# Two-head scores in the halves of the array, softmax sums dividing y, and six w buffers in a decoder layer

## The chip, the cores and the metric

The kernel runs on one core of a Trainium2 chip. The metric is the device time of one execution in microseconds (us); the median of the runs is compared. Engines are named as in the profile: PE is the matrix engine (TensorE), PEld its weight loads, DVE VectorE, ACT ScalarE, POOL GpSimd, SP the engine that issues nearly all DMAs.

## The reference

One decoder layer on x[1024 x 1024], float32. A combined input projection feeds three branches, whose outputs are concatenated and projected back; a gated MLP (ConvFFN) and a last norm follow. Cut to what matters here:

```
h = rmsnorm(x);  p = h @ w_in
# 6 "fox" heads of 64: causal, with a decay bias c_q - c_k
s = q @ k.T * 64**-0.5 + c_q - c_k;  s = where(k <= q, s, -inf)
ya = rmsnorm(softmax(s) @ v)
# 6 dilated heads of 64: three windows (128,1), (512,4), (2048,16) mixed by their sums:
# a softmax over all keys with a fixed table added to the scores
yb = rmsnorm(dilated_mixture(q, k, v))
# 256 channels, 31 taps
yc = silu(layernorm(causal_dwconv(gv * sigmoid(gg), conv_w) + conv_b))
x = x + concat(ya, yb, yc) @ w_o
```

## The kernel before, in words

Every matmul whose operands are float32 is made of three products of high and low parts (hi·hi, lo·hi, hi·lo); a helper issues them as L116, L117 and L118. Activations lie transposed, features on the partitions. The attention stage, about 125 to 527 us of the span, goes over six pairs of heads (pair 0 to 2 fox, 3 to 5 dilated). For each pair a generator `attention` goes over four blocks of 256 queries (i) and both heads (h): `scores` makes two tiles w[128 queries x up to 1024 keys], in chunks of at most 512 keys: two matmuls into a PSUM slot (L379, L380; fox adds a mask, L382), a DVE operation that adds the bias and takes the minimum (L385, since q is negated), the exponential with its row sum on ACT (L390), then the reciprocal of the sum on DVE (L392) and the division of w on POOL (L393). `turn` transposes w (L405) and splits it into hi and lo (L409 on ACT, L410 on DVE), `values` multiplies with V (L421, L422), and L444, L445 add the two halves into y. PSUM has five slots for scores and transposes together, SBUF four buffers (tag "sp") for w.

L379 contracts over 128 rows: QA holds the 64 rows of a head's q_hi and under them its q_lo, KA twice k_hi. L380 contracts over 64 rows, q_hi with k_lo (in KL).

A mixer, `mix`, draws units of other matmul work (the projections of the next pair, norms, the first output projections) between the steps of `attention`, by weights given to each step. The order on each engine is fixed when the program is built: a scheduler goes through the instructions by their dependences, by priority and by when it expects buffers to come free, and each engine then runs its list in order.

The convolution (`conv_taps`) is written behind pair 0: one DVE operation per channel block starts the sum (L506) and 30 more each add a tap (L508), into yc0 and yc1, which have buffers of their own. Its norm (`conv_norm`) is mixed into pair 1. yc is needed again behind pair 4, where it is split for the output projection.

```
yc = [bp.tile([P, S], F32, tag=f"yc{c}", name=f"yc{c}") for c in range(2)]
...
V.tensor_scalar(y, u, col(wc + 30), col(C_CB + c), op0=ALU.mult, op1=ALU.add)
for d in range(1, 31):
    V.scalar_tensor_tensor(y[:, d:], u[:, 0:S - d], col(wc + 30 - d), y[:, d:],
                           op0=ALU.mult, op1=ALU.add)
```

Of the kernel before, what the change touches and what calls it, by code (L numbers as in the profile page):

```python
# [60 lines left out]
def hybrid_trunk(ctx: ExitStack, tc: tile.TileContext, xT, par, win, wvf, wo, wup, wdn,  # L61
# [88 lines left out]
    with ExitStack() as cb_:  # L150
# [70 lines left out]
        V.tensor_copy(idb, idf)  # L221

        V.tensor_scalar(mkb, trf, -BIG, BIG, op0=ALU.mult, op1=ALU.add)
# [16 lines left out]
        yc = [bp.tile([P, S], F32, tag=f"yc{c}", name=f"yc{c}") for c in range(2)]  # L240
# [43 lines left out]
        def proj_q(pr, out):  # L284
            QA, QB = pair_tile(f"QA{pr}"), pair_tile(f"QB{pr}")
            out["Q"] = (QA, QB)
            w = load_chunk(win[pr if pr < 3 else pr + 3], 8, f"wq{pr}")
            for i in range(2):
                ps = mm_ps(f"qps{pr}_{i}")
                yield from mm_gen(ps, w, xs, HS[i])  # L290
                qs = bp.tile([P, HALF], F32, tag="ev", name=f"qs{pr}_{i}", bufs=2)
                V.scalar_tensor_tensor(qs, ps, -0.125, r1b[:, HS[i]], op0=ALU.mult, op1=ALU.mult)
                h = HS[i]
                A.copy(QA[0:64, h], qs[0:64])
                A.copy(QB[64:128, h], qs[64:128])
                G.tensor_sub(QA[64:128, h], qs[0:64], QA[0:64, h].bitcast(F32))
                G.tensor_sub(QB[0:64, h], qs[64:128], QB[64:128, h].bitcast(F32))

        def proj_k(pr, out):
            KA = pair_tile(f"KA{pr}")  # L300
            if pr in (2, 4):
                kk = bp.tile([P, 2, S], F32R, tag="VS", name=f"KBL{pr}", bufs=3)
                KB, KL = kk[:, 0, :], kk[:, 1, :]
            else:
                KB, KL = pair_tile(f"KB{pr}"), pair_tile(f"KL{pr}")
            out["K"], out["KL"] = (KA, KB), KL
            w = load_chunk(win[pr + 3 if pr < 3 else pr + 6], 8, f"wk{pr}")
            for i in range(2):
# [8 lines left out]
                A.copy(KA[0:64, h], ks[0:64])  # L317
                A.copy(KB[64:128, h], ks[64:128])
                G.tensor_scalar(KA[64:128, h], ks[0:64], 1.0, 0.0, op0=ALU.mult, op1=ALU.add)
                G.tensor_scalar(KB[0:64, h], ks[64:128], 1.0, 0.0, op0=ALU.mult, op1=ALU.add)  # L320
                V.tensor_sub(KL[0:64, h], ks[0:64], KA[0:64, h].bitcast(F32))
                V.tensor_sub(KL[64:128, h], ks[64:128], KB[64:128, h].bitcast(F32))
# [35 lines left out]
        def attention(pr, a, bias, fox, y, ahead):  # L358
            Q, K, KL, VSp = a["Q"], a["K"], a["KL"], a["V"]
            steps = [(i, h) for i in range(NT // 2) for h in range(2)]  # L360
            ws = {}

            def scores(n):
                i, h = steps[n]
                ro = slice(64 * h, 64 * h + 64)
                nm = f"{pr}_{i}_{h}"
                ws[n] = []
                for j in range(2):
                    qi = 2 * i + j
                    nk = P * (qi + 1)  # L370
                    qsl = slice(P * qi, nk)
                    w = sp_tile(f"w{nm}_{j}")
                    mn = None
                    for c0 in range(0, nk, HALF):
                        m = min(HALF, nk - c0)
                        ks = slice(c0, c0 + m)
                        ps = s_ps(f"s{nm}_{j}_{c0}")
                        diag = fox and c0 + m == nk
                        T.matmul(ps[:, 0:m], lhsT=Q[h][:, qsl], rhs=K[h][:, ks], start=True, stop=False)  # L379
                        T.matmul(ps[:, 0:m], lhsT=Q[h][ro, qsl], rhs=KL[ro, ks], start=False, stop=not diag)  # L380
                        if diag:
                            T.matmul(ps[:, m - P:m], lhsT=mkb, rhs=idb, start=False, stop=True)  # L382
                        m2 = bp.tile([P, 1], F32, tag="mn", name=f"mn{nm}_{j}_{c0}", bufs=8)
                        b = bias[h][:, ks] if fox else bias[h][:, S - nk + c0:S - nk + c0 + m]
                        V.tensor_tensor_reduce(out=w[:, ks], in0=ps[:, 0:m], in1=b, scale=1.0,  # L385
                                               scalar=3.0e38 if mn is None else mn,
                                               op0=ALU.add, op1=ALU.min, accum_out=m2)
                        mn = m2
                    den = bp.tile([P, 1], F32, tag="den", name=f"den{nm}_{j}", bufs=4)
                    A.activation(w[:, 0:nk], w[:, 0:nk], AF.Exp, scale=-1.0, bias=mn, accum_out=den)  # L390
# [35 lines left out]
            for n, (i, h) in enumerate(steps):  # L426
# [893 lines left out]
```

## Time and profile before

| | |
|---|---|
| median of 3 runs (lowest to highest) | 1322.84 us (1322.1 to 1322.9) |
| the profiled execution: its own time / its span | 1320.88 us / 1319.1 us |
| PE busy, whole span | 1240.6 us (94%) |
| DVE / ACT / POOL busy | 1062.8 / 635.9 / 602.6 us |
| granted TensorE clock, mean | 0.973 |

The span is the profiled part of that execution. Busy times are sums over instructions; matmuls overlap each other in the pipeline, so the price of a matmul is better read from the distance between the starts of neighbours.

### The profile page before, as it was taken

What the parts mean: (1) busy time and instruction counts of PE and PEld (TensorE: products, weight loads), DVE (VectorE), ACT (ScalarE), POOL (GpSimd) and SP (SyncE); (2) the same over time, 40 slices, a digit from 0 to 9 for tenths busy, and PEclk for the clock granted to TensorE, in tenths of its full rate; (3) what the DMA queues carried; (4) which work ended last, traced back from release to release, by engine and by line L of the source; (5) the groups of instructions that cost most, each with busy time, mean ns of one, the idle gap of its engine ahead of it and who ended that gap; (6) DMA issues with size and microseconds to landing.
All of it is one profiled execution on the core that took longest, in us unless ns stands there. A gap on an engine that the chain in (4) does not pass through costs nothing.

```text
span 1319.1 us, 17062 instructions
## 1 busy us (share of the span) xinstructions
PE 1240.6 (94%) x5809; PEld 987.8 (75%) x5809; DVE 1062.8 (81%) x1589; ACT 635.9 (48%) x1146; POOL 602.6 (46%) x517
## 2 busy tenths in 40 slices
PE   7899899999999999998697999999999979999996
PEld 5887677777777767775476888888888858787795
DVE  8799797756665576789989888888888898978876
ACT  6413456566555564425344455544554554534333
POOL 4566455643655342357751111111111375767754
PEclk9999899999999999998798999999999989999998
DMA  7002010101000112220022323313332454535213
GB/s 236 21 17 81 9 56 18 48 17 49 17 18 28 42 33 100 76 95 16 0 81 104 112 104 112 112 70 111 104 116 104 129 190 147 188 92 160 64 31 128
DMA packets 56407, 106.69 MB, mean 81 GB/s; under 512 B 5456, under 2 KB 25600, under 8 KB 56320
## 3 DMA queue, kind: packets, MB, share of 16 engines
q1 hardware_dynamic: 55744, 105.32, 23.7%
q8 instruction: 46, 0.75, 0.2%
q14 instruction: 41, 0.34, 0.1%
q10 hardware_dynamic: 576, 0.28, 0.1%
HBM read 82.75 MB, written 22.83 MB: 80 GB/s over the span
## 4 chain that ended last, share of the span: by engine, by line
PE 65%; DVE 20%; POOL 5%; issue 5%; DMA 3%; ACT 2%; SPq 0%; DVEq 0%; ACTq 0%; POOLq 0%
PE mA L116 5%; PE mA L117 5%; PE mA L118 5%; PE m L118 4%; PE m L117 4%; PE m L116 4%; PE s L380 4%; PE pt L405 3%; PE d L118 3%; PE d L117 3%; PE d L116 3%; PE s L379 3%; DVE yc L508 3%; PE av L422 2%; PE av L421 2%
## 5 line engine op out<-in xcount | busy, mean ns | idle before, releaser
L828 POOL TENSOR_TENSOR wl<-a,wh 128x512 fp32r<-128x512 f32 x48 | 69.7, 1453 | 294.6 <-ACT wh L827 282.4
L393 POOL TENSOR_SCALAR w<-w,rd 128x128 f32<-128x128 f32 (+3 forms) x96 | 77.0, 806 | 137.7 <-DVE rd L392 80.9
L118 PE MATMUL d<-hc,wld 128*128 128x512 f32 x252 | 101.8, 404 | 7.9 <-POOL wld L828 7.9
L410 DVE TENSOR_TENSOR pl<-pt,ph 128x512 fp32r<-128x512 f32 (+1 forms) x120 | 74.9, 634 | 38.6 <-ACT ph L409 35.5
L117 PE MATMUL d<-hc,whd 128*128 128x512 f32 x252 | 100.4, 398 | 5.3 <-DVE hc L1146 5.3
L390 ACT ACTIVATE w<-w,mn 128x128 f32<-128x128 f32 (+3 forms) x96 | 74.4, 775 | 61.6 <-DVE mn L385 58.5
L116 PE MATMUL d<-hc,whd 128*128 128x512 f32 x252 | 100.2, 398 | 0.8 <-ACT whd L827 0.8
L117 PE MATMUL m<-t,wh 128*128 128x512 f32 x208 | 83.0, 399 | 7.5 <-DVE t L741 7.5
L508 DVE SCALAR_TENSOR_TENSOR yc<-gv,prm,yc 128x1023 f32<-128x1023 f32 (+29 forms) x60 | 89.0, 1483 | 0.9
L116 PE MATMUL m<-t,wh 128*128 128x512 f32 x208 | 82.2, 395 | 4.2 <-ACT t L740 4.2
L409 ACT CAST ph<-pt 128x512 fp32r<-128x512 f32 (+1 forms) x120 | 63.8, 541 | 44.6 <-PE pt L405 31.8
L118 PE MATMUL m<-t,wl 128*128 128x512 f32 x208 | 82.5, 397 | 1.4 <-POOL wl L828 1.4
L405 PE MATMUL pt<-idf,w 128*128 128x128 f32 x432 | 70.8, 279 | 8.1 <-POOL w L393 7.7
L827 ACT CAST wh<-a 128x512 fp32r<-128x512 f32 x84 | 52.2, 621 | 41.5 <-issue 24.3
L828 POOL TENSOR_TENSOR wld<-a_d,whd 128x384 fp32r<-128x384 f32 x48 | 57.3, 1196 | 21.4 <-ACT whd L827 21.3
L118 PEld LDWEIGHTS d<-hc,wld 128*128 128x128 f32 x252 | 48.5, 193 | 23.7 <-POOL wld L828 13.9
L422 PE MATMUL av<-pl,VS 128*128 128x256 f32 x240 | 61.1, 289 | 3.2 <-DVE pl L410 3.2
L421 PE MATMUL av<-ph,VS 128*128 128x256 f32 x240 | 63.8, 285 | 0.2
L116 PE MATMUL mA<-t,wh 128*128 128x512 f32 x144 | 56.9, 395 | 6.4 <-ACT u L1034 6.4
L405 PEld LDWEIGHTS pt<-idf,w 128*128 128x128 f32 x432 | 50.4, 142 | 15.7 <-POOL w L393 11.1
L828 DVE TENSOR_TENSOR wl<-s,wh 128x512 fp32r<-128x512 f32 x54 | 42.9, 795 | 22.7 <-ACT wh L827 22.7
L117 PEld LDWEIGHTS d<-hc,whd 128*128 128x128 f32 x252 | 48.5, 192 | 16.8 <-DVE hc L1146 6.4
(465 smaller groups left out, 4035.7 us busy)
## 6 DMA issues: line engine op xcount, KB each, us to landing
a<-in_wup SPq DMA_DIRECT2D x88, 256.0 KB, 2.7
tr<-td SPq DMA_DIRECT2D x27, 512.0 KB, 3.8
a_d<-in_wdn SPq DMA_DIRECT2D x48, 192.0 KB, 2.4
td<-cv SPq DMA_DIRECT2D x9, 512.0 KB, 2.6
td<-ta SPq DMA_DIRECT2D x9, 512.0 KB, 3.5
td<-tb SPq DMA_DIRECT2D x9, 512.0 KB, 3.6
x<-in_xT SPq DMA_DIRECT2D x8, 512.0 KB, 3.7
outT<-fo SPq DMA_DIRECT2D x8, 512.0 KB, 3.0
```

What stands on the lines that cost most here:

```text
L116: T.matmul(ps, lhsT=wh, rhs=xh[:, sl], start=first, stop=False, **kw)
L117: T.matmul(ps, lhsT=wh, rhs=xl[:, sl], start=False, stop=False, **kw)
L118: T.matmul(ps, lhsT=wl, rhs=xh[:, sl], start=False, stop=last, **kw)
L390: A.activation(w[:, 0:nk], w[:, 0:nk], AF.Exp, scale=-1.0, bias=mn, accum_out=den)
L393: G.tensor_scalar(w[:, 0:nk], w[:, 0:nk], rd, 1.0, op0=ALU.mult, op1=ALU.mult)
L405: T.transpose(pt[:, P * b:P * b + P], ws[n][j][:, P * kt:P * kt + P], idf)
L409: A.copy(ph[:, 0:w], pt[:, 0:w])
L410: V.tensor_sub(pl[:, 0:w], pt[:, 0:w], ph[:, 0:w].bitcast(F32))
L421: T.matmul(o, lhsT=vt, rhs=phl[0][:, r], start=kt == 0, stop=False)
L422: T.matmul(o, lhsT=vt, rhs=phl[1][:, r], start=False, stop=kt == 2 * i + 1)
L508: V.scalar_tensor_tensor(y[:, d:], u[:, 0:S - d], col(wc + 30 - d), y[:, d:], op0=ALU.mult, op1=ALU.add)
L828: eng.tensor_sub(lo, t, hi.bitcast(F32))
```

## The change

Four things are changed.

1. Q and K of a pair are kept as QH, QL, KH, KL, both heads one above the other (64 rows each). `scores(qi)` now makes one block of 128 queries for both heads: three products for each head, all over 64 rows, head 0 in the upper and head 1 in the lower rows, in turn. Each chunk takes two PSUM slots. The mask is two 64-row matmuls for each head.
2. w is no longer divided. The row sums are kept in `den`; `sums` takes the reciprocals of four blocks and two heads at once, transposes them and stores them to DRAM; `divide` loads them back, spread over the partitions, and multiplies 256 columns of y by them on DVE. L392 and L393 are gone.
3. The tag "sp" has six buffers instead of four, and yc0 and yc1 are taken from it too. yc is stored to DRAM after pair 1 and loaded into two "sp" tiles behind pair 4. From pair 2 on, the next scores are written before the transposes of the step instead of behind them.
4. KL is computed on POOL with the full 128 rows, and the weights of the mixer are new.

```diff
-            return bp.tile(shape or [P, S], dt, tag="sp", name=name, bufs=4)
+            return bp.tile(shape or [P, S], dt, tag="sp", name=name, bufs=6)
...
-        yc = [bp.tile([P, S], F32, tag=f"yc{c}", name=f"yc{c}") for c in range(2)]
+        yc = [sp_tile(f"yc{c}") for c in range(2)]
...
-                G.tensor_sub(QA[64:128, h], qs[0:64], QA[0:64, h].bitcast(F32))
-                G.tensor_sub(QB[0:64, h], qs[64:128], QB[64:128, h].bitcast(F32))
+                A.copy(QH[:, h], qs)
+                G.tensor_sub(QL[:, h], qs, QH[:, h].bitcast(F32))
...
-                V.tensor_sub(KL[0:64, h], ks[0:64], KA[0:64, h].bitcast(F32))
-                V.tensor_sub(KL[64:128, h], ks[64:128], KB[64:128, h].bitcast(F32))
+                A.copy(KH[:, h], ks)
+                G.tensor_sub(KL[:, h], ks, KH[:, h].bitcast(F32))
...
-                        T.matmul(ps[:, 0:m], lhsT=Q[h][:, qsl], rhs=K[h][:, ks], start=True, stop=False)
-                        T.matmul(ps[:, 0:m], lhsT=Q[h][ro, qsl], rhs=KL[ro, ks], start=False, stop=not diag)
+                    ps = [s_ps(f"s{nm}_{h}") for h in range(2)]
+                    terms = ((QH, KH), (QL, KH), (QH, KL))
+                    for n, (q, k) in enumerate(terms):
+                        for h, ro in heads:
+                            T.matmul(ps[h][:, 0:m], lhsT=q[ro, qsl], rhs=k[ro, ks],
+                                     start=n == 0, stop=n == 2 and not diag)
...
-                    V.reciprocal(rd, den)
-                    G.tensor_scalar(w[:, 0:nk], w[:, 0:nk], rd, 1.0, op0=ALU.mult, op1=ALU.mult)
...
+            def sums(f):
+
+                V.reciprocal(den[f], den[f])
+                tp = pt_ps(f"rdp{pr}_{f}")
+                T.transpose(tp[0:8, 0:P], den[f], idf)
+                row = bp.tile([8, P], F32, tag="tr", name=f"row{pr}_{f}", bufs=1)
+                A.copy(row, tp[0:8, 0:P])
+                nc.sync.dma_start(rdd[pr][f], row)
+
+            def divide(i):
+
+                r = bp.tile([P, 256], F32, tag="rdb", name=f"rdb{pr}_{i}", bufs=1)
+                for h in range(2):
+                    n = 4 * h + 2 * (i % 2)
+                    src = rdd[pr][i // 2][n:n + 2].rearrange("(o a) s -> o (a s)", o=1)
+                    nc.sync.dma_start(r[64 * h:64 * h + 64], src.broadcast_to([64, 256]))
+                yi = y[:, 256 * i:256 * i + 256]
+                return lambda: V.tensor_mul(yi, yi, r)
...
+                if i < NT // 2 - 1 and pr >= 2:
+                    yield from scores(2 * i + 2 + h)
...
-                if n + 2 < len(steps):
-                    yield from scores(n + 2)
-                values(n, i, av, prev)
+                if i < NT // 2 - 1 and pr < 2:
+                    yield from scores(2 * i + 2 + h)
+                values(i, h, i, av, prev)
...
+            if pr == 1:
+                for c in range(2):
+                    nc.sync.dma_start(ycd[c], yc[c])
             if pr == 4:
                 for c in range(2):
-                    split(6 + c, yc[c])
+                    t = sp_tile(f"ycr{c}")
+                    nc.sync.dma_start(t, ycd[c])
+                    split(6 + c, t)
```

The changed program's own line numbers appear in the pieces of order below; there L376 is the score matmul, L386 the bias and minimum, L422 the transposes, L427 the split, L437 and L438 the products with V, L467 the sum into y, L413 the division of y, L531 and L533 the convolution.

On DVE the taps of the convolution stood one by one between other work before, here in pair 0 (yc is the sum, gv its input, rd the reciprocal, pl a low part of a transposed w):

```order
L508 SCALAR_TENSOR_TENSOR yc_327<-gv_317,prm,yc_327 128x1010
L445 TENSOR_TENSOR y_958<-av_0_0_1035,yt_0_0_1078 64x256
L392 RECIPROCAL rd_1_0_0_1056<-den_1_0_0_1054 128x1
L392 RECIPROCAL rd_1_0_1_1068<-den_1_0_1_1066 128x1
L410 TENSOR_TENSOR pl_0_1_0_1087<-pt_0_1_0_1082,ph_0_1_0_1086 128x384
L385 ISA w_1_1_0_1093,mn_1_1_0_0_1098<-s_1_1_0_0_1094,cb_961 128x384
L385 ISA mn_1_1_0_0_1098 128x1
L385 ISA w_1_1_1_1105,mn_1_1_1_0_1110<-s_1_1_1_0_1106,cb_961 128x512
L385 ISA mn_1_1_1_0_1110 128x1
L508 SCALAR_TENSOR_TENSOR yc_327<-gv_317,prm,yc_327 128x1009
```

In the changed program none stands in pair 0. The first two rows of the convolution follow the first reduces of pair 1 (w_0_0 and w_0_1), and 60 taps come from there on; this is where they begin:

```order
L386 ISA w_0_1_1605,mn_0_0_1_1620<-s_0_0_1_1607,cb_1600 128x128
L386 ISA mn_0_0_1_1620 128x1
L531 TENSOR_SCALAR yc_334<-gv_324,prm 128x1024
L531 TENSOR_SCALAR yc_335<-gv_325,prm 128x1024
L427 TENSOR_TENSOR pl_3_1_2_1634<-pt_3_1_2_1628,ph_3_1_2_1633 128x512
L427 TENSOR_TENSOR pl_3_1_3_1646<-pt_3_1_3_1641,ph_3_1_3_1645 128x384
L533 SCALAR_TENSOR_TENSOR yc_334<-gv_324,prm,yc_334 128x1023
L467 TENSOR_TENSOR y_967<-av_3_1_1562,yt_3_1_1657 64x256
L533 SCALAR_TENSOR_TENSOR yc_334<-gv_324,prm,yc_334 128x1022
L413 TENSOR_TENSOR y_967<-y_967,rdb_3_1661 128x256
L533 SCALAR_TENSOR_TENSOR yc_334<-gv_324,prm,yc_334 128x1021
L533 SCALAR_TENSOR_TENSOR yc_335<-gv_325,prm,yc_335 128x1023
```

Behind the last row of it only taps follow, 56 of them, up to the reduce of w_1_0 (the second block of queries, head 0); this is where they end:

```order
L533 SCALAR_TENSOR_TENSOR yc_334<-gv_324,prm,yc_334 128x994
L533 SCALAR_TENSOR_TENSOR yc_335<-gv_325,prm,yc_335 128x996
L386 ISA w_1_0_1727,mn_1_0_0_1741<-s_1_0_0_1729,cb_1598 128x256
L386 ISA mn_1_0_0_1741 128x1
L533 SCALAR_TENSOR_TENSOR yc_335<-gv_325,prm,yc_335 128x995
L386 ISA w_1_1_1728,mn_1_0_1_1743<-s_1_0_1_1730,cb_1600 128x256
L386 ISA mn_1_0_1_1743 128x1
L533 SCALAR_TENSOR_TENSOR yc_335<-gv_325,prm,yc_335 128x994
```

On PE at the same place the second half of the query projection of the next pair (qps_1) ends, and the first transposes of pair 1 follow. pt_0_1_0 takes a PSUM slot that the reduce of w_1_0 sets free, and pt_0_0_0 reads w_1_0 itself:

```order
L118 MATMUL qps_1_1922<-xh_264,wh_wq_4_1757 128x512
L119 MATMUL qps_1_1922<-xl_265,wh_wq_4_1757 128x512
L120 MATMUL qps_1_1922<-xh_264,wl_wq_4_1758 128x512
L422 MATMUL pt_0_1_0_1808<-idf,w_0_1_1605 128x128
L422 MATMUL pt_0_0_0_1766<-idf,w_1_0_1727 128x128 x2
L376 MATMUL s_3_0_0_1821<-KH_1325,QH_994 128x512
L437 MATMUL av_0_0_1765<-ph_0_0_0_1770,VS_362 128x256
```

Between the reduces of w_0 and of w_1 DVE now has the convolution, and PE's transposes stand behind those reduces.

The scores on PE, in pair 5: before, a chunk of one head was a product over 128 rows and one over 64.

```order
L379 MATMUL s_2_0_0_0_4912<-KA_4519,QA_4002 128x512
L380 MATMUL s_2_0_0_0_4912<-KL_4521,QA_4002 128x512
L379 MATMUL s_2_0_0_512_4917<-KA_4519,QA_4002 128x128
L380 MATMUL s_2_0_0_512_4917<-KL_4521,QA_4002 128x128
L379 MATMUL s_2_0_1_0_4928<-KA_4519,QA_4002 128x512
L380 MATMUL s_2_0_1_0_4928<-KL_4521,QA_4002 128x512
```

Now a chunk of two heads is six products over 64 rows, the heads in turn, often with a second chunk right behind (the name ends in the head):

```order
L376 MATMUL s_6_0_0_4255<-KH_3750,QH_3239 128x512
L376 MATMUL s_6_0_1_4256<-KH_3750,QH_3239 128x512
L376 MATMUL s_6_0_0_4255<-KH_3750,QL_3240 128x512
L376 MATMUL s_6_0_1_4256<-KH_3750,QL_3240 128x512
L376 MATMUL s_6_0_0_4255<-KL_3751,QH_3239 128x512
L376 MATMUL s_6_0_1_4256<-KL_3751,QH_3239 128x512
L376 MATMUL s_6_512_0_4267<-KH_3750,QH_3239 128x384
L376 MATMUL s_6_512_1_4268<-KH_3750,QH_3239 128x384
```

Six score matmuls over 64 rows stand where four stood, two of them over 128.

## Rows read from the trace of the kernel before

**Rows 1.** The page's sums: busy time, share and instructions by engine.

```profile
PE 1240.6 (94%) x5809; PEld 987.8 (75%) x5809; DVE 1062.8 (81%) x1589; ACT 635.9 (48%) x1146; POOL 602.6 (46%) x517
```

**Rows 2.** Stretches: length, busy PE, PEld, DVE, ACT, POOL, clock, DMA, GB/s.

```profile
125.00:195.00 70.00, 64.07 (x321) 46.81 (x320) 60.95 (x121) 34.32 (x75) 38.33 (x33) 0.93 0.12 38
195.00:520.00 325.00, 319.48 (x1616) 238.84 (x1616) 211.98 (x528) 186.72 (x384) 155.21 (x159) 0.99 0.11 35
```

**Rows 3.** Timeline of PE from 405 us: start, duration, line, operands.

```profile
405.14 0.34 PE L379 MATMUL s<-KA,QA 128*128 128x384 f32 x1
405.41 0.44 PE L380 MATMUL s<-KBL,QA 64*128 64x384 f32 x1
405.78 0.50 PE L379 MATMUL s<-KA,QA 128*128 128x512 f32 x1
406.21 0.49 PE L380 MATMUL s<-KBL,QA 64*128 64x512 f32 x1
406.63 0.50 PE L116 MATMUL qps<-xh,wh_wq 128*128 128x512 f32 x1
406.96 0.40 PE L117 MATMUL qps<-xl,wh_wq 128*128 128x512 f32 x1
407.20 0.39 PE L118 MATMUL qps<-xh,wl_wq 128*128 128x512 f32 x1
...
407.54 0.28 PE L422 MATMUL av<-pl,VS 128*128 128x256 f32 x1
407.66 0.22 PE L421 MATMUL av<-ph,VS 128*128 128x128 f32 x1
407.72 0.28 PE L422 MATMUL av<-pl,VS 128*128 128x128 f32 x1
```

**Rows 4.** Timeline of PE from 397 us.

```profile
397.10 0.22 PE L379 MATMUL s<-KA,QA 128*128 128x128 f32 x1
397.25 0.32 PE L380 MATMUL s<-KBL,QA 64*128 64x128 f32 x1
397.51 0.39 PE L379 MATMUL s<-KA,QA 128*128 128x256 f32 x1
397.82 0.38 PE L380 MATMUL s<-KBL,QA 64*128 64x256 f32 x1
398.14 0.38 PE L421 MATMUL av<-ph,VS 128*128 128x256 f32 x1
```

**Rows 5.** Groups of DVE, 40 to 206 us: busy, mean ns, idle before.

```profile
L508 DVE SCALAR_TENSOR_TENSOR yc<-gv,prm,yc 128x1023 f32<-128x1023 f32 (+29 forms) x60 | 89.0, 1483 | 0.9
...
L506 DVE TENSOR_SCALAR yc<-gv,prm 128x1024 f32<-128x1024 f32 x2 | 1.6, 811 | 0.1
```

**Rows 6.** Timeline of DVE, two places of the convolution.

```profile
92.30 1.25 DVE L508 SCALAR_TENSOR_TENSOR yc<-gv,prm,yc 128x998 f32<-128x998 f32 x1
93.47 0.19 DVE L473 SCALAR_TENSOR_TENSOR lf_p<-lf_p,lf_t 128x48 f32<-128x48 f32 x1
...
115.38 6.54 DVE L508 SCALAR_TENSOR_TENSOR yc<-gv,prm,yc 128x1018 f32<-128x1018 f32 x3
```

**Rows 7.** Timeline of PE, pair 0; in brackets the idle time and its releaser.

```profile
130.59 0.40 PE L118 MATMUL qps<-xh,wl_wq 128*128 128x512 f32 x1
135.13 0.48 PE L405 MATMUL pt<-idf,w 128*128 128x128 f32 x1 [4.14 <-POOL w L393]
...
136.64 0.69 PE L405 MATMUL pt<-idf,w 128*128 128x128 f32 x2 [0.71 <-POOL w L393]
```

**Rows 8.** The stretch behind that wait, columns as in rows 2.

```profile
134.00:144.00 10.00, 8.16 (x24) 5.20 (x24) 6.13 (x20) 3.74 (x11) 3.36 (x6) 0.51 0.00 0
```

**Rows 9.** Groups of the whole span: division, exponential, reduce (dilated pairs).

```profile
L393 POOL TENSOR_SCALAR w<-w,rd 128x128 f32<-128x128 f32 (+3 forms) x96 | 77.0, 806 | 137.7 <-DVE rd L392 80.9 <-PE pt L405 35.4 <-ACT w L390 11.2
...
L390 ACT ACTIVATE w<-w,mn 128x128 f32<-128x128 f32 (+3 forms) x96 | 74.4, 775 | 61.6 <-DVE mn L385 58.5 <-POOL wl_wv L103 2.1 <-DVE rd L392 0.6
...
L385 DVE CUSTOM_DVE_ANT_0 w<-s,dil_tab 128x512 f32<-128x512 f32 (+3 forms) x48 | 28.1, 588 | 19.1 <-PE s L380 17.3 <-POOL QB L297 0.8 <-POOL wl_woc L103 0.2
```

**Rows 10.** DMA issues: KB each, us from issue to landing.

```profile
x<-in_xT SPq DMA_DIRECT2D x8, 512.0 KB, 3.7
```

More of the change, by code (lines that the diff above doesn't have):

```diff
@@ L27 @@
 BIG = 1e30
-W0, W1 = 1, 0.3
-WT = (1.4, 1.8, 1.4, 2.2, 0.2)
-AHEAD = (7, 1), 2
+WS = (2, 2, 0.6, 2, 0.6, 2, 0.6, 2)
+WT = (1.4, 1.0, 1.8, 1.4, 1.4, 1.4, 2.2, 0.2)
+TOTAL = sum(WS) + sum((n // 2 + 1) * w for n, w in enumerate(WT))
+AHEAD = (3, 1, 1), 2
 F1 = (9, 12, 14, 18, 21, 23, 27, 30)
@@ L219, in hybrid_trunk @@
             half_rsqrt(r1b[:, HS[i]], ps, D, f"r1{i}")
-        V.tensor_copy(idb, idf)
-        V.tensor_scalar(mkb, trf, -BIG, BIG, op0=ALU.mult, op1=ALU.add)
+        for r in range(2):
+            for to in range(2):
+                src, dst = slice(64 * r, 64 * r + 64), slice(64 * to, 64 * to + 64)
+                V.tensor_copy(idb[r][dst], idf[src])
+                V.tensor_scalar(mkb[r][dst], trf[src], -BIG, BIG, op0=ALU.mult, op1=ALU.add)
         r1c = bp.tile([P, NT], F32, name="r1c")
@@ L358, in attention @@
         def attention(pr, a, bias, fox, y, ahead):
-            Q, K, KL, VSp = a["Q"], a["K"], a["KL"], a["V"]
+            (QH, QL), (KH, KL), VSp = a["Q"], a["K"], a["V"]
             steps = [(i, h) for i in range(NT // 2) for h in range(2)]
[L361 to L378, printed above, removed]
-                        T.matmul(ps[:, 0:m], lhsT=Q[h][:, qsl], rhs=K[h][:, ks], start=True, stop=False)
-                        T.matmul(ps[:, 0:m], lhsT=Q[h][ro, qsl], rhs=KL[ro, ks], start=False, stop=not diag)
-                        if diag:
-                            T.matmul(ps[:, m - P:m], lhsT=mkb, rhs=idb, start=False, stop=True)
-                        m2 = bp.tile([P, 1], F32, tag="mn", name=f"mn{nm}_{j}_{c0}", bufs=8)
@@ new lines, in attention, with scores @@
+            ws, todo = {}, []
+            den = [bp.tile([P, 8], F32, tag="den", name=f"den{pr}_{f}", bufs=3) for f in range(2)]
+            def scores(qi):
+                nk = P * (qi + 1)
+                qsl = slice(P * qi, nk)
+                heads = [(h, slice(64 * h, 64 * h + 64)) for h in range(2)]
+                mn = [None, None]
+                for h, _ in heads:
+                    ws[qi, h] = sp_tile(f"w{pr}_{qi}_{h}")
+                for c0 in range(0, nk, HALF):
+                    m = min(HALF, nk - c0)
+                    ks = slice(c0, c0 + m)
+                    nm = f"{pr}_{qi}_{c0}"
+                    ps = [s_ps(f"s{nm}_{h}") for h in range(2)]
+                    diag = fox and c0 + m == nk
+                    terms = ((QH, KH), (QL, KH), (QH, KL))
[3 more added lines that the diff above has]
+                                     start=n == 0, stop=n == 2 and not diag)
+                    if diag:
+                        for r in range(2):
+                            for h, ro in heads:
+                                T.matmul(ps[h][:, m - P:m], lhsT=mkb[r][ro], rhs=idb[r][ro],
+                                         start=False, stop=r == 1)
+                    for h, _ in heads:
+                        m2 = bp.tile([P, 1], F32, tag="mn", name=f"mn{nm}_{h}", bufs=8)
@@ L450, in mix @@
             for weight in main:
[L451 removed]
+                due += weight * units / TOTAL
                 while due >= 1:
@@ L590, in out1 @@
                 V.tensor_add(x1[e][:, HS[i]], ps, x1[e][:, HS[i]])
+        rdd = [[dram.tile([8, P], F32, name=f"rdd{pr}_{f}") for f in range(2)] for pr in range(6)]
+        ycd = [dram.tile([P, S], F32, name=f"ycd{c}") for c in range(2)]
         gate_mul(0)
@@ L657, in ahead @@
                     mains[pr + 1] = start(pr + 1)
-                    for _ in range(AHEAD[1]):
+                    for _ in range(AHEAD[1] if pr else 1):
                         yield next(mains[pr + 1])
```

67 lines of the change are left out of this document (30 added, 37 removed).

## The prediction

> **What bounds the kernel now.** I read the page's sums first: PE is busy for 94% of the span, DVE for 81%, ACT and POOL for under half [rows 1]. That is an average, so next the stretches of the attention stage, the only one that the change touches. From 195 to 520 us PE is busy for 319.48 of 325 us at a clock of 0.99, while DVE has 113 us to spare, ACT 138 and POOL 170 [rows 2]. There only PE's work and PE's waits count; work taken from the other three is worth nothing. From 125 to 195 us PE lacks 6 us and the clock is 0.93 [rows 2]. The timeline shows why: after the matmul at 130.59 PE waits 4.14 us, and once more 0.71 us, for a w that POOL has to divide [rows 7], and in the 10 us behind it the clock is 0.51, that is the lower of its two levels, 1.2 GHz [rows 8]. So a wait costs more than its length.
>
> **The scores on PE.** Prices are distances between starts. Two neighbouring 512-column matmuls over 128 rows start 0.24 us apart (406.96 to 407.20) [rows 3]; I take 0.23, since a 256-column one takes 0.12 and a 128-column one 0.06 (407.54 to 407.66 to 407.72) [rows 3]; 384 columns are then 0.17. A pair L379, L380, behind another such pair, takes 0.85 us for 512 columns (405.78 to 406.63) [rows 3], where two plain matmuls would take 0.46. The matmul behind it takes 0.33 instead of 0.24 to its neighbour [rows 3], so going back from 64 rows to 128 shows 0.10 us there, and the pair that starts behind a pair holds that 0.10 too. Without it a pair costs 0.75 for 512 columns, 0.64 for 384 (405.14 to 405.78, behind a plain matmul) [rows 3], 0.63 − 0.10 = 0.53 for 256 and 0.41 for 128 [rows 4]. One excursion from 128 rows to 64 and back is therefore 0.75 + 0.10 − 0.46 = 0.39 us more than its columns.
>
> Before there are 144 chunks (72 of 512 columns, 24 each of 384, 256 and 128): 72 × 0.75 + 24 × (0.64 + 0.53 + 0.41) + 144 × 0.10 = 106.3 us. After, 72 two-head chunks (36, 12, 12, 12) of three products for each head, with 88 unbroken runs of 64-row matmuls in PE's order. What a 64-row matmul costs when its neighbour uses the other half of the array no row shows. If the halves work at the same time, a pair of products costs one: 36 × 3 × 0.23 + 12 × 3 × (0.17 + 0.12 + 0.06) = 37.4 us, with 88 × 0.39 = 34.3 it is 71.8: **34.5 us saved**. If they don't, the columns cost 74.9, in all 109: 3 us lost. L380 is near a plain matmul in duration (0.49 against 0.50) [rows 3], which says nothing about two at once. I take the overlap: the two use different rows, different operands and different PSUM slots. The widths agree on an excursion (256: 0.53 + 0.10 − 0.24 = 0.39; 128: 0.41 + 0.10 − 0.12 = 0.39), so I hold it for the same in longer runs. Bounds: 60 saved (if of an excursion only the 0.10 stayed, 37.4 + 8.8) to 3 lost.
>
> The Trainium skill bears on both ends (TensorEngine Tiling (Array Packing), Key Properties): different tiles of the array can load weights and multiply at once, and a change of the tiling mode drains the engine. The trace agrees with the second, 0.39 us for each excursion; the first no run here shows. By it the sum is the 34.5 us saved above, without it 3 us lost.
>
> **The taps.** Before, the 60 taps stand one by one between DVE's other work, 89.0 us of it [rows 5], and hide behind PE's work. Now yc0 and yc1 come out of the six "sp" buffers, which w tiles of pair 0 hold until their transposes are done. So in the changed order no tap stands in pair 0; two start rows and two taps come behind the first reduces of pair 1, and then 56 taps in a row stand ahead of the reduce of w_1_0. Behind that reduce are the other reduces, and behind those, on ACT and PE, the exponential of w_1, the transposes pt_0_1_0 and pt_0_0_0, and all of PE's list. PE's list has little to put there: the second projection of q, 48 matmuls × 0.23 = 11.0 us, and the scores of block 2, about 1: 12 us.
>
> How long the block lasts: the operation behind a tap, which doesn't depend on it, starts 1.17 us after it (92.30 to 93.47) [rows 6]. 57 × 1.17 = 66.7 (56 taps and one start row at most in the way). With the addition and the division of y of 256 columns each (0.4 us each, from the reduce's 588 ns at a mean of 384 columns [rows 9]), the reduce itself (0.45), an exponential (0.775 on average [rows 9]) and 2 us for POOL beside it, about two of its weight splits (three taps beside POOL's work took 6.54 us [rows 6], 3.0 more than 3 × 1.17) the block is 71 us. Less 12 us: **PE waits 59 us**. Then the clock: before, a wait of 4.14 us was followed by 10 us at 0.51 [rows 8], which is 5 us lost; I add 5. The term is +64. Upper bound: at the mean tap of 1.483 us [rows 5], 57 × 0.31 = 18 more. Lower bound: 57 taps at the 0.811 us of the start row [rows 5], a single-input operation and the cheapest of that size, 20 less.
>
> **What pair 0 gets back.** With no taps there, a w is ready sooner, and the division by POOL is gone: the 4.14 and 0.71 us of waiting [rows 7] and the 5 us of the low clock [rows 8] go, −10 (bounds −5 to −15, since other waits of 125 to 195 us may stay or go).
>
> **PSUM slots.** A two-head chunk takes two of the five slots, and DVE has to reduce both. A call with two chunks brings four reduces: 4 × 0.588 [rows 9] with the read-outs about 2.7 us, while PE gives it 1.0 to 1.4 us of columns, 0.39 of excursion and what stands mixed between. Most of the gap is filled by projections; +4 (0 to 31: 24 such calls at 1.3 us, which is 2.7 less the 1.4).
>
> **The y division and the queues.** L393's 77.0 us on POOL [rows 9] and L392 on DVE go, worth nothing behind PE. Instead there are 24 multiplies of y, and each second one must wait for a load that its predecessor's end allows (one rdb buffer). 11 to 24 DVE operations stand between the two in the order, at 0.4 to 0.6 us each at least 4.4 us, while 512 KB take 3.7 us to land [rows 10] and this is 64 KB twice; hidden, and if the cover is gone 12 × 3.7 us at most. The store, the two loads and the wait stand on SP ahead of weight loads; these feed the matmuls of the next projection, a projection or a half ahead: nothing.
>
> **yc back from DRAM.** At the end of pair 4 the reload waits for free "sp" buffers, and the output projection of pair 5 begins with it: one landing of 3.7 us [rows 10] and a cast of 1024 columns on ACT (0.775 × 1024/576 = 1.4 [rows 9], 576 being the mean width) are 5.1, **+5** (0 if mixed work covers it, 9 if both tiles land one after the other). KL on POOL and the new mixing weights cost nothing as long as PE is the bound.
>
> **Sum.** 1320.88 − 34.5 − 10 + 64 + 4 + 5 = 1349.4; the profiled execution is 1.96 us below the median, so against the median it is **1351 us** (+2.1%). A difference of 0.2%, 2.6 us, is about the least that can be told from none here.
>
> **Rivals.** *The halves don't overlap* (the change does not do what it says for PE): 3 us lost instead of 34.5 saved, so 1351 + 37.5 = 1388. For it: no row shows two 64-row matmuls side by side. Against: nothing that they share.
>
> *DVE's reduces set the pace of the scores*: one chunk now brings two reduces at once, and PE waits for slots. At the whole +31 instead of +4: 1378; at half of it, 1363. For it: reduces of 0.588 us [rows 9] against 0.46 us of halves; against: DVE's spare 113 us [rows 2] and mixed matmuls. The skill's same page (PSUM Bottleneck) warns of this: tiling speeds the matrix engine, not what empties PSUM. Here DVE's idle time in front of the reduce, 19.1 us, is mostly spent waiting for PE [rows 9]; the reverse no row shows yet.
>
> *The block is short, and the kernel is not slower.* The taps of the block alternate between yc0 and yc1, so each is independent of the one before. If that let them follow at under 1.17 us, the term shrinks by 57 us for each us. All other terms save 34.5 + 10 − 4 − 5 = 35.5; the block term is 57s + 4 − 12 + 5, which is 35.5 at s = 0.68 us. At 0.60 it is 31.2: 1320.88 − 35.5 + 31.2 = 1316.6, and 1318.6 against the median. For it: nothing but the 0.811 us of the start row [rows 5], itself too slow. Against: an independent operation had to wait 1.17 us too.
>
> **Chances.** Forecast 0.66, own range 1334 to 1366 (the block at 1.17 us with 15 us either way for its bounds and those of the scores); no overlap 0.15; reduces 0.10; short block 0.05; something else 0.04, half of it faster. The range 1334 to 1390 leaves out the short block and some of the first rival's upper half, together under 2 in 10. Faster 0.06, same 0.02, slower 0.92.
>
> **What the profile after would show.** Taps only from the start of pair 1 on, 56 in a row at about 1.17 us; a wait of PE of some 59 us ahead of a transpose, released by the reduce or the exponential of w_1, then some 10 us at 0.5 clock; no 4.14 us wait in pair 0; L376 matmuls of the two heads starting in pairs, 0.23 us a pair; PE's busy time some 30 us lower. The prediction is wrong if the taps are spread, if the L376 matmuls start 0.23 us apart each, or if PE waits for reduces in every burst.

## The result and the profile after

The changed kernel takes 1370.07 us (median of 4 runs, 1368.36 to 1371.68) against 1322.47 us of the kernel before (1321.25 to 1322.9): a ratio of 1.0361, 95% interval 1.0343 to 1.0379. It is 47.6 us slower; 1351 was predicted, 28 us slower, with a range of 1334 to 1390.

The page's sums of the kernel after, engine by engine (busy time, share, instructions), to be held against [rows 1]:

```profile
span 1366.6 us, 17153 instructions
...
PE 1224.1 (90%) x6013; PEld 984.6 (72%) x6013; DVE 1022.5 (75%) x1511; ACT 619.6 (45%) x1134; POOL 534.2 (39%) x397
```

Every engine has less to do than before, PE 16.5 us less (some 30 were predicted), and the span is 47.5 us longer: time went into waiting. What PE waited for, over the whole span (total, times, longest):

```profile
PE pt L422 <- DVE mn L386: 57.5, 4, 55.2
PE av L437 <- ACT ph L426: 11.3, 13, 2.7
```

The first row is one wait of 55.2 us. The timeline of PE shows it between the query projection and the first transposes of pair 1, the place of [rows 7] one pair later:

```profile
195.29 0.39 PE L120 MATMUL qps<-xh,wl_wq 128*128 128x512 f32 x1
250.90 1.23 PE L422 MATMUL pt<-idf,w 128*128 128x128 f32 x3 [55.22 <-DVE mn L386]
252.86 0.79 PE L376 MATMUL s<-KH,QH 64*128 64x512 f32 x1 [0.73 <-DVE mn L386]
```

DVE in the same stretch, its start and its end; where a row has x5 or x7 it stands for so many taps in a row:

```profile
184.13 6.05 DVE L533 SCALAR_TENSOR_TENSOR yc<-gv,prm,yc 128x1021 f32<-128x1021 f32 x5
...
242.04 8.25 DVE L533 SCALAR_TENSOR_TENSOR yc<-gv,prm,yc 128x999 f32<-128x999 f32 x7
250.32 0.42 DVE L386 CUSTOM_DVE_ANT_0 w<-s,cb 128x256 f32<-128x256 f32 x1
250.67 0.08 DVE L386 DVE_READ_ACCUMULATOR2_ANT mn<- 128x1 f32 x1
```

From 184.13, the tap of 1021 columns, to 250.32 DVE does nothing but 56 taps, 1.18 us each; the reduce of w_1_0 stands behind them, and PE goes on when it has read out. The windows show the price beside the wait (columns as in [rows 2]; the second and third answer to [rows 8]):

```profile
195.00:260.00 65.00, 8.95 (x28) 5.28 (x28) 64.12 (x66) 5.78 (x15) 61.16 (x4) 0.53 0.02 8
250.00:260.00 10.00, 8.27 (x25) 5.06 (x26) 9.12 (x20) 5.17 (x14) 6.16 (x4) 0.50 0.15 52
260.00:270.00 10.00, 10.00 (x57) 7.47 (x56) 4.61 (x15) 4.47 (x11) 1.27 (x1) 0.81 0.05 15
```

PE is busy for 9 of 65 us, and the clock is 0.50 for 10 us behind the wait and 0.81 for 10 more. As an estimate from these shares, 10 × 0.50 + 10 × 0.19 = 6.9 us are lost by it.

The scores did get cheaper. Timeline of PE in pair 3; "x2" stands for the matmuls of the two heads, which start within 0.01 us of each other:

```profile
399.77 0.51 PE L376 MATMUL s<-KH,QH 64*128 64x512 f32 x2
400.11 0.39 PE L376 MATMUL s<-KH,QL 64*128 64x512 f32 x2
400.34 0.39 PE L376 MATMUL s<-KL,QH 64*128 64x512 f32 x2
400.56 0.28 PE L376 MATMUL s<-KH,QH 64*128 64x256 f32 x2
400.68 0.28 PE L376 MATMUL s<-KH,QL 64*128 64x256 f32 x2
400.80 0.28 PE L376 MATMUL s<-KL,QH 64*128 64x256 f32 x2
401.01 0.50 PE L118 MATMUL qps<-xh,wh_wq 128*128 128x512 f32 x1
401.34 0.40 PE L119 MATMUL qps<-xl,wh_wq 128*128 128x512 f32 x1
401.58 0.39 PE L120 MATMUL qps<-xh,wl_wq 128*128 128x512 f32 x1
```

A pair of 512-column products takes 0.23 us (400.11 to 400.34) and one of 256 takes 0.12, as much as one matmul alone. The price of going back to 128 rows is where it was: 0.33 instead of 0.24 us for the first projection matmul. The way from 128 rows to 64 has a price too, and it shows on the matmul that stands ahead of the scores:

```profile
407.61 0.23 PE L437 MATMUL av<-ph,VS 128*128 128x128 f32 x1
407.67 0.27 PE L438 MATMUL av<-pl,VS 128*128 128x128 f32 x1
407.88 0.50 PE L376 MATMUL s<-KH,QH 64*128 64x512 f32 x2
```

A product with V of 128 columns is 0.06 us from its neighbour over 128 rows (407.61 to 407.67), and 0.21 from a score matmul over 64 (407.67 to 407.88). Before, that way lay inside a pair, between L379 and L380.

To see where the stage's time went I added up the distances between the starts of neighbouring matmuls on PE, by kind, from the first query projection to the last output projection of the stage (us; e1 is the first experiment below; waits, and the way from 128 rows to 64, are in the kind that stands ahead of them):

| | before | after | e1 |
|---|---|---|---|
| scores | 102.2 | 69.9 | 66.2 |
| mask | 2.0 | 8.3 | 6.4 |
| products with V | 64.0 | 71.8 | 70.7 |
| transposes of the sums | 0 | 2.7 | 2.8 |
| projections | 249.0 | 310.3 | 258.2 |
| transposes of w, norms, the rest | 52.1 | 53.8 | 50.8 |
| sum | 469.3 | 516.8 | 455.1 |

### The profile page after: what moved, and what is told of

Read it like the earlier page. It is cut to its first block, busy times and chain, and to the rows that moved or that the text cites. A ratio compares the mean times of both kernels' runs of the same rounds, so it can differ in the third digit from the quotient of the medians.

```text
span 1366.6 us, 17153 instructions
## 1 busy us (share of the span) xinstructions
PE 1224.1 (90%) x6013; PEld 984.6 (72%) x6013; DVE 1022.5 (75%) x1511; ACT 619.6 (45%) x1134; POOL 534.2 (39%) x397
## 4 chain that ended last, share of the span: by engine, by line
PE 43%; DVE 10%; DMA 2%; issue 2%; POOL 2%; ACT 1%; DVEq 0%; POOLq 0%; ACTq 0%
PE mA L118 5%; PE mA L120 5%; PE mA L119 5%; PE m L120 4%; PE m L118 4%; PE m L119 4%; PE d L120 3%; PE d L119 3%; PE d L118 3%; DMA tr<-td 2%; PE dl L120 1%; PE dl L119 1%; PE dl L118 1%; POOL wld L860 1%; DVE hc L1178 1%
## 5 line engine op out<-in xcount | busy, mean ns | idle before, releaser
L392 ACT ACTIVATE w<-w,mn 128x128 f32<-128x128 f32 (+7 forms) x96 | 73.9, 771 | 102.9 <-DVE mn L386 102.2
L427 DVE TENSOR_TENSOR pl<-pt,ph 128x512 fp32r<-128x512 f32 (+1 forms) x120 | 73.8, 634 | 61.4 <-ACT ph L426 61.2
L422 PE MATMUL pt<-idf,w 128*128 128x128 f32 x432 | 67.9, 277 | 57.8 <-DVE mn L386 57.5
L105 POOL TENSOR_TENSOR wl_wk<-raw_wk,wh_wk 128x512 fp32r<-128x512 f32 x12 | 72.1, 6006 | 73.5 <-ACT wh_wk L104 71.1
L422 PEld LDWEIGHTS pt<-idf,w 128*128 128x128 f32 x432 | 51.2, 141 | 67.5 <-issue 56.8
L437 PE MATMUL av<-ph,VS 128*128 128x256 f32 x240 | 65.9, 293 | 11.7 <-ACT ph L426 11.3
L533 DVE SCALAR_TENSOR_TENSOR yc<-gv,prm,yc 128x1023 f32<-128x1023 f32 (+29 forms) x60 | 72.4, 1282 | 0.0
L120 PEld LDWEIGHTS d<-hc,wld 128*128 128x128 f32 x252 | 48.4, 192 | 24.1 <-POOL wld L860 14.4
L438 PE MATMUL av<-pl,VS 128*128 128x256 f32 x240 | 63.6, 302 | 1.6 <-DVE pl L427 1.6
L437 PEld LDWEIGHTS av<-ph,VS 128*128 128x128 f32 x240 | 46.2, 193 | 23.4 <-ACT ph L426 19.7
```

Of the source, the lines that this page charges most:

```text
L105: G.tensor_sub(lo[:, 0:kt], raw[:, 0:kt], hi[:, 0:kt].bitcast(F32))
L120: T.matmul(ps, lhsT=wl, rhs=xh[:, sl], start=False, stop=last, **kw)
L422: T.transpose(pt[:, P * b:P * b + P], ws[2 * i + j, h][:, P * kt:P * kt + P], idf)
L427: V.tensor_sub(pl[:, 0:w], pt[:, 0:w], ph[:, 0:w].bitcast(F32))
L437: T.matmul(o, lhsT=vt, rhs=phl[0][:, r], start=kt == 0, stop=False)
L438: T.matmul(o, lhsT=vt, rhs=phl[1][:, r], start=False, stop=kt == 2 * i + 1)
```

## The experiments

Theory A: the whole loss is the block of taps, which the shared "sp" buffers make; the two-head scores gain. The rivals put the loss, or what is missing of the gain, into the scores' halves, the four or six buffers, or the new waits for ACT. Ratios are to the kernel before, run beside each.

**e1, the convolution's starts ahead of pair 0.** Only the first writers of yc0 and yc1 move; the taps' lines stay behind pair 0.

```diff
         gate_mul(0)
         gates1()
         gate_mul(1)
+        for c in range(2):
+            conv_start(c)
...
-        def conv_taps(c):
+        def conv_start(c):
             wc, u, y = C_CW + 31 * c, us[c], yc[c]
             V.tensor_scalar(y, u, col(wc + 30), col(C_CB + c), op0=ALU.mult, op1=ALU.add)
+
+        def conv_taps(c):
+            wc, u, y = C_CW + 31 * c, us[c], yc[c]
```

> The changed kernel with one thing moved: the two operations that start the convolution's sums (the first writers of yc0 and yc1) are written ahead of pair 0, the 60 taps stay where they were. yc then holds two of the six buffers from before pair 0, and the taps are free to stand between pair 0's work. Theory A (the block of 56 taps is the loss): PE's wait of 55.2 us and its 0.7 us successor go, and with them the low clock behind them, about 8 us; the kernel takes 1370 - 64 = 1306 us, faster than before by 1.2%. Rival B (the block only gathers waits that the two-head scores and the four remaining buffers bring anyway): the taps among pair 0's work bring back the 10 us of waits that before had there, and w tiles run short; 1320 us or more, no better than before.

Measured: 1310.82 us, ratio 0.9911 (0.9892 to 0.9931). The summary of the taps' line in e1 (duration least/median/most, first and last start):

```profile
L536 DVE SCALAR_TENSOR_TENSOR yc<-gv,prm,yc x60: 1162/1278/2299, 53.8 to 179.0; 128x1023 f32<-128x1023 f32 x2, 128x1022 f32<-128x1022 f32 x2, 128x1021 f32<-128x1021 f32 x2, 128x1020 f32<-128x1020 f32 x2
```

The taps are spread over 125 us again (in after their first and last start are 180.7 and 252.7), the 55.2 us wait is gone, and the change becomes a gain of 0.9%. Theory A holds: 1.0361 − 0.9911 is 0.045, some 59 us. The time is 5 us above the 1306 expected.

**e2, the heads one after the other.**

```diff
-                    for n, (q, k) in enumerate(terms):
-                        for h, ro in heads:
+                    for h, ro in heads:
+                        for n, (q, k) in enumerate(terms):
                             T.matmul(ps[h][:, 0:m], lhsT=q[ro, qsl], rhs=k[ro, ks],
```

> The changed kernel with the two loops of the score products exchanged: all three products of head 0, then all three of head 1, so that neighbours mostly use the same half of the array. Theory A (neighbours in different halves work at the same time, which gives the 37 us of columns that the scores save): 24 us or more are lost, since of three pairs only the one in the middle still has neighbours of different halves; between 1370 + 20 = 1390 and 1370 + 37 = 1407 us. Rival (what was saved is the way from 128 rows to 64 and back, and the order of the heads does not matter): 1370 us.

Measured: 1369.48 us, 1.0372 (1.0345 to 1.0399), the same as after. My expectation was a miss, and the trace of e2 shows why it tells nothing against the overlap:

```profile
398.50 0.50 PE L376 MATMUL s<-KH,QH 64*128 64x512 f32 x2
398.84 0.39 PE L376 MATMUL s<-KH,QL 64*128 64x512 f32 x2
399.07 0.40 PE L376 MATMUL s<-KL,QH 64*128 64x512 f32 x2
```

PE's list has head 0 three times, then head 1 three times; but the first product of head 1 starts beside the first of head 0, at 398.51 beside 398.50, ahead of two that stand before it in the list. This holds for most of them: 322 of the 432 score matmuls of e2 start within 0.03 us of another one, and 360 of 432 in after. The sentence ahead of the prediction that each engine runs its list in order is therefore too simple for PE; over three instructions the order hardly matters here.

**e3, the block alone, in the kernel before.**

```diff
-            return bp.tile(shape or [P, S], dt, tag="sp", name=name, bufs=4)
+            return bp.tile(shape or [P, S], dt, tag="sp", name=name, bufs=6)
...
-        yc = [bp.tile([P, S], F32, tag=f"yc{c}", name=f"yc{c}") for c in range(2)]
+        yc = [sp_tile(f"yc{c}") for c in range(2)]
```

> The kernel before with yc0 and yc1 taken from the sp buffers, of which there are six; nothing else of the change. In its order 60 taps and starts stand nearly in one block at the start of pair 1. Theory A: this edit alone brings the wait of some 55 us and the low clock behind it, less up to 10 us of pair 0's waits, so 1322 + 55 = 1377 us (1365 to 1390). Rival C (the block costs that much only because the two-head scores leave PE so little to do beside it): under 1345 us.

Measured: 1371.74 us, 1.038 (1.036 to 1.04). Two lines that save no memory and change no arithmetic cost as much as the whole change. PE's waits in e3:

```profile
PE pt L405 <- POOL w L393: 63.5, 3, 61.7
```

Here the division on POOL stands behind the exponential and is named as the releaser, but it is the same wait behind the same taps: the reduce comes at 253.25, and only the last 3.7 us, up to 256.93, go to the exponential, the reciprocal and the division. Rival C falls. e3 also shows what pair 0 had waited for. The taps are gone from there and the division is still in place, and PE waits only once, 0.33 us, where [rows 2] had 64.07 us of work at a clock of 0.93:

```profile
125.00:195.00 70.00, 69.54 (x364) 52.20 (x363) 50.49 (x113) 34.92 (x74) 28.59 (x32) 1.00 0.10 31
```

**e4 and e8, the buffers, the trip of yc and the early scores.** e4 goes back to four "sp" buffers and yc's own, without store and reload, and writes all scores late; e8 is e1 with all scores late.

```diff
-                if i < NT // 2 - 1 and pr >= 2:
+                if i < NT // 2 - 1 and pr >= 9:
                     yield from scores(2 * i + 2 + h)
...
-                if i < NT // 2 - 1 and pr < 2:
+                if i < NT // 2 - 1 and pr < 9:
                     yield from scores(2 * i + 2 + h)
```

> The changed kernel with yc in buffers of its own, four sp buffers as before, no trip of yc through DRAM, and no scores written a step early: what is left are the two-head scores, the division of y and KL on POOL. Theory A: no block, and no reload of yc: 1306 - 3 = 1303 us if the early scores are worth nothing. Rival D (the early scores and the six buffers are what keeps PE fed from pair 2 on): 1 to 2 us for each of the 24 two-block steps of pairs 2 to 5 are lost, 1303 + 30 = 1333 us.

> The kernel of e1 without the scores written a step early from pair 2 on; the six buffers, the trip of yc through DRAM and all else stay. Theory A (early scores only move PE's work, and PE has other work in its list either way): within 3 us of 1311. Rival D (with late scores the transposes come up before their exponential is done): 3 to 15 us more, up to 1326, with PE waits for w at the transposes; e4, with late scores, was at 1314.

Measured: e4 1314.02 us, 0.9943 (0.9928 to 0.9958); e8 1317.98 us, 0.9979 (0.9966 to 0.9993). e4 lies between its two forecasts (1303 and 1333). From e1 to e8 the ratio rises by 0.0068: the early scores are worth 9 us, rival D. From e8 to e4 it falls by 0.0036: yc in "sp" with its trip through DRAM, against four buffers and yc's own, costs 4.8 us where scores are late, give or take 3. PE's waits in e8 from 98 to 575 us show a part of what late scores bring:

```profile
PE av L437 <- ACT ph L426: 8.3, 15, 1.8
PE pt L422 <- ACT w L392: 6.1, 6, 2.0
PE rdp L400 <- DVE den L398: 5.4, 7, 2.2
```

In e1 these were 11.7, 3.9 and 1.2: PE waits longer for the exponentials and the sums and less for the split. Over the whole stage its waits rise by 3.5 us, from 25.4 to 28.9. The rest of the 9 us lies in distances without a wait and is not traced further.

**e5, one half for both heads.** From e1; head 1 computes head 0's scores, so part of the output is that of other scores.

```diff
-                            T.matmul(ps[h][:, 0:m], lhsT=q[ro, qsl], rhs=k[ro, ks],
+                            T.matmul(ps[h][:, 0:m], lhsT=q[0:64, qsl], rhs=k[0:64, ks],
...
-                                T.matmul(ps[h][:, m - P:m], lhsT=mkb[r][ro], rhs=idb[r][ro],
+                                T.matmul(ps[h][:, m - P:m], lhsT=mkb[r][0:64], rhs=idb[r][0:64],
```

> The kernel of e1 (the convolution's starts ahead of pair 0), in which the scores of head 1 are computed from the rows of head 0, so that every score product and mask uses the same half of the array; the output is then not the reference's. All counts, sizes, slots and the order of work stay. Theory A (in e2 the two halves still started together, since each half takes its matmuls from the list on its own): with one half alone the columns count twice, 36 x 3 x 0.23 + 12 x 3 x 0.35 = 37 us more on PE; some 8 us of that fill waits that PE has beside the scores; 1311 + 30 to 37 = 1341 to 1348 us. Rival (the saving comes from fewer changes between 128 and 64 rows): 1311 us.

Measured: 1337.13 us, 1.0113 (1.0092 to 1.0135), 0.0202 or 27 us above e1. The same sum over PE's starts as above gives 98.7 us for the scores, 32.5 more than in e1. The overlap of the halves is real, and it is the whole saving: with the way from 128 rows to 64, 11.3 us in e5 and 0.7 in before, the scores over one half cost 110 us, against 103 before. The time is a little under the 1341 to 1348 expected: 6 of the 32.5 us are found again in waits that this longer work covers (PE waits 3.8 us for the split instead of 11.7).

**e6, the division alone**, put into the kernel before: w undivided, `sums` and `divide` as in the change (the diff's part 2, with the calls at the second head of each second block), all else of before.

```diff
-                    rd = bp.tile([P, 1], F32, tag="rd", name=f"rd{nm}_{j}", bufs=4)
-                    V.reciprocal(rd, den)
-                    G.tensor_scalar(w[:, 0:nk], w[:, 0:nk], rd, 1.0, op0=ALU.mult, op1=ALU.mult)
...
+                if (i % 2, h) == (1, 1):
+                    sums(i // 2)
+                    todo.append(divide(i - 1))
```

> The kernel before with the sums dividing y instead of w, and nothing else of the change: scores, buffers and the mixer's weights are those of before. Gone are 96 reciprocals on DVE and 96 divisions on POOL, new are 12 transposes, 12 stores, 48 loads and 24 multiplies of y. Theory A: PE waited 7.7 us for POOL's division in before; these go, with the low clock behind the longest, and 12 transposes of the sums cost about 0.23 us each: 1322 - 8 - 4 + 3 = 1313 us. Rival E (the waits move to the exponential, which stands ahead of the division, and the loads of the sums hold up DVE): 1322 us or more.

Measured: 1317.53 us, 0.9971 (0.9957 to 0.9986): 4 us gained, less than half of the 9 that theory A had. PE's waits in e6:

```profile
PE pt L422 <- ACT w L409: 3.4, 1, 3.4
PE av L439 <- DVE pl L427: 3.4, 2, 2.1
```

Of the 4.14 us of [rows 7] 3.4 stay, now for the exponential: POOL's division was the last in that chain, not its reason. 77 us of POOL's work went, and the kernel got some 4 us.

**e7, the split first**, from e1.

```diff
-                A.copy(ph[:, 0:w], pt[:, 0:w])
-                V.tensor_sub(pl[:, 0:w], pt[:, 0:w], ph[:, 0:w].bitcast(F32))
+                with tc.high_priority():
+                    A.copy(ph[:, 0:w], pt[:, 0:w])
+                    V.tensor_sub(pl[:, 0:w], pt[:, 0:w], ph[:, 0:w].bitcast(F32))
```

> The kernel of e1 with the split of the transposed w (on ACT and DVE) at high priority, so that ACT's list has it ahead of exponentials and casts that are ready at the same time. In e1 PE waits 11.7 us in 15 places for that split on ACT. Theory A: ACT's order is what makes these waits, most of them go: 1311 - 8 = 1303 us. Rival F (the split waits behind work that has already begun, or the wait turns into one for the exponentials that are pushed back): 1311 us or more.

Measured: 1304.45 us, 0.9875 (0.9859 to 0.9892), the fastest of all. PE's waits in the stage, of e1 first:

```profile
PE av L437 <- ACT ph L426: 11.7, 15, 2.7
PE pt L422 <- ACT w L392: 3.9, 3, 2.0
```

and of e7:

```profile
PE av L438 <- ACT ph L427: 6.3, 10, 2.4
PE pt L422 <- ACT w L392: 5.1, 4, 3.0
```

Waits for the split fall by 5.4 us, those for the exponential rise by 1.2: theory A for most of it, some of F. What stands ahead of the split, the timeline of ACT in after shows at the longest of these waits, 2.7 us: the exponentials of both heads, one behind the other.

```profile
378.44 0.49 ACT L392 ACTIVATE w<-w,mn 128x256 f32<-128x256 f32 x1
378.83 0.19 ACT L392 ACTIVATION_READ_ACCUMULATOR w<-w,mn 128x1 f32 x1
378.93 0.49 ACT L392 ACTIVATE w<-w,mn 128x256 f32<-128x256 f32 x1
379.33 0.18 ACT L392 ACTIVATION_READ_ACCUMULATOR w<-w,mn 128x1 f32 x1
379.42 0.93 ACT L426 CAST ph<-pt 128x512 fp32r<-128x512 f32 x2
```

**e9 and e10, that priority with yc's own buffers, and in the kernel before.** e9 is e4 with the scores early from pair 2 on and e7's edit; e10 is the kernel before with e7's edit alone.

> The changed kernel with yc in buffers of its own, four sp buffers, no trip of yc through DRAM, the scores still written a step early from pair 2 on, and the split of the transposed w at high priority (as in e7). Theory A (e4 was 3.6 per mille below e8, which is the same kernel with yc in the sp buffers and the trip through DRAM; the early scores gave 7 per mille): 1304 - 5 = 1299 us. Rival G (six buffers are what lets the early scores be early; with four, the next scores' reduces wait for the transposes of the step, and PE has the early matmuls for nothing): like late scores, 1304 + 4 = 1308 us or more.

> The kernel before with the split of the transposed w at high priority and nothing else. In before PE does not wait for ACT's half of that split at all (its waits in the attention stage are 7.7 us for POOL's division and 3.2 us for DVE's half of the split). Theory A (the waits for ACT that e7 removed come with the two-head scores, whose two exponentials and reduces arrive together): no gain, 1321 us within 3. Rival H (the priority is worth as much without the change): 1321 - 6 = 1315 us.

Measured: e9 1312.63 us, 0.9927 (0.9903 to 0.995), slower than e7: the time is in rival G's range. With six buffers the early scores and the priority together lowered the ratio by 0.0104 (e8 to e7), with four by 0.0016 (e4 to e9). G's mechanism is not seen, though: PE waits for 20.0 us of the stage in e9 and 22.5 in e7. What grew is the distances without a wait, 440.5 against 428.4 us, and 110 score matmuls start alone instead of 64. e10 1328.87 us, 1.0057 (1.0036 to 1.0078): rival H falls, and it is even slower than expected. PE's waits in e10:

```profile
PE pt L405 <- POOL w L393: 14.4, 8, 5.2
```

PE waits 14.4 us for a divided w where it waited 7.7; that the exponentials, pushed back on ACT by the split, are the reason is likely, but was not shown. What the priority gives in e7 it gives only beside the rest of the change.

## Why the prediction was right

**The number** came out within the stated range by some luck. The range that the forecast gave its own mechanism was 1334 to 1366; 1370 lies above that, in the part that was added for two rivals, heads that don't overlap and reduces that set the pace, and both of them fall. The block, the wait and the overlap were right; the sizes of the rest were not.

**The block** was right in place, cause and size: 56 taps in a row, 1.18 us each (1.17 predicted), a wait of 55.2 us (59), and some 6.9 us of low clock behind it (5): with the 0.7 us of a second wait 55.2 + 0.7 + 6.9 = 62.8 against 64. e1 takes the block away and gets 59 us back; e3 puts it into the kernel before and loses 50. Of the 4 us too much of the wait, 2 are those for POOL, which did not slow the taps, and 2 are PE's list, which lasted 13.9 us (181.79 to 195.68) instead of 12.

**The scores on PE** were right in mechanism. The two heads overlap, 0.23 us a pair, and e5 shows that the overlap carries the saving. The Trainium skill's rule that different tiles work in parallel (TensorEngine Tiling (Array Packing), Key Properties) now has its row: pairs of starts within 0.01 us. The rival that denied it falls, as does the one of the short block: alternating accumulators left a tap at 1.18 us.

**What was mis-sized** is the rest. Without the block term the sum had −35.5 us; e1 is 0.0089 or 12 us below before, and after without its block (1370.1 − 62.8 = 1307.3) is 15 below. The distances between PE's starts show where the 20 us went that are missing in after. Its waits outside the block are 23.5 us against 13.4 before, 10 more, where the sum had 4 more (4 for the slots and 5 for yc, less the 4.85 of pair 0). Its distances without a wait, less the 6.9 us of low clock, fall by 25 us, where the sum had 39.5 (34.5 for the scores, 5 for the clock in pair 0). So 6 of the 20 us are waits and 14 are PE's own work:

- *The waits for ACT were put at nothing.* The +4 for PSUM slots and reduces was nearly right: 2.3 us at three transposes and 0.7 at a score matmul. PE also waits 11.3 us for the split of the transposed w on ACT, because two exponentials now arrive together and stand ahead of it; before it had no such wait. e7 gets about half of it back by order alone. The Trainium skill's warning that what empties PSUM may become the limit (TensorEngine Tiling (Array Packing), PSUM Bottleneck) has the 3.0 us for the reduces to show here. The split reads PSUM as well, but it was late by ACT's order.
- *The scores' term* of −34.5. The table's 102.2 to 69.9 us looks like 32.3 saved, but the way from 128 rows to 64 now stands in other kinds, 12.8 us of it: ahead of the 88 runs of 64-row matmuls stands a product with V 54 times, a projection matmul 21 times and a transpose 11 times. That is why the products with V cost 7.8 us more; their waits got fewer. With this way and without waits the scores went from 102.2 to 75.0 us, 27 saved, part of it measured at the low clock behind the block. The sum took each product to start beside its partner; 72 of the 432 start alone.
- *The mask*, which I did not price: 96 matmuls of 64 rows for 48 of 128, 6.3 us more (8.3 against 2.0), 1.0 of it a wait; 4.4 in e1.
- *The 12 transposes of the sums*, not priced either: 2.7 us on PE, 1.1 of it a wait for DVE's reciprocal.

In PE's own work that is 7 + 5 + 2 = 14 us, as near as it can be divided: the way back to 128 rows stands in the kind behind and is not counted here. What the new weights of the mixer and KL on POOL do by themselves no run shows.

**Pair 0's waits** of [rows 7] did go in after: from 125 to 195 us PE is busy for 66.63 us at a clock of 0.98, against 64.07 at 0.93 [rows 2]. But that gain hangs on the missing taps, not on the division: e1, with the taps back, waits 2.0 and 1.6 us there, e6, without the division, keeps 3.4, and e3, with the division and without the taps, waits 0.33. I had put it down to both, and counted it rightly only for a kernel that pays for it with the block.

**yc through DRAM** was priced at +5; e8 to e4 shows 4.8, with the buffers' number changed along with it. The wait that I had given as the reason is not there: PE's waits of the stage are 28.9 us in e8 and 29.7 in e4, so the agreement is luck. The early scores, 9 us by e1 and e8, I had not priced at all. That e6 would keep most of pair 0's wait was not foreseen either. One reading was off without consequence: the 588 ns of [rows 9] belong to a mean of 416 columns (30 reduces of 512 and 6 each of 384, 256 and 128), not 384.

## What to carry to other kernels

A shared pool of buffers is also a schedule: when two long-lived tiles join a ring that short-lived ones fill, all work on them waits for the ring and then comes at once; look in the order for where the first writer of such a tile lands. Moving that first writer by a few lines was worth 59 us here. Making the matrix engine faster by joining two heads makes everything behind it arrive in twos, so the order on the engine that comes next (here ACT) has to be set anew; with both repairs the change gains 1.25%. When you read a price from distances between starts, look at the kind ahead as well: a change of shape is paid there.

## What the hardware showed that I had not expected

While DVE ran its 56 taps, one POOL operation, of a kind that takes 1.3 to 2.2 us elsewhere, took 57.90 us, and in e3, beside that block, 61.25 us. Timeline of POOL in after, the same kind of operation twice:

```profile
193.51 57.90 POOL L105 TENSOR_TENSOR wl_wk<-raw_wk,wh_wk 128x512 fp32r<-128x512 f32 x1 [14.40 <-ACT wh_wk L104]
251.37 2.22 POOL L105 TENSOR_TENSOR wl_wq<-raw_wq,wh_wq 128x512 fp32r<-128x512 f32 x1
```

It ended 1.1 us after the start of the first operation that broke the row of taps (250.32). The taps themselves kept 1.18 us, where in before three taps beside POOL's work had taken 6.54 us [rows 6]. So in the block POOL was held up and DVE was not; what decides this was not tried. PE did not wait for this POOL operation in after.

The two halves of the array take matmuls out of the list's order: in e2 head 1's first product started 0.01 us behind head 0's (398.51 and 398.50), past two that stood ahead of it.
